# A written order for TensorE and VectorE in the recurrence loop of a hybrid trunk layer

## The chip, the cores and the metric

The kernel runs on one core of a Trainium2 chip. The metric is device time in microseconds (us) for one launch. TensorE is called PE below, VectorE DVE, ScalarE ACT, GpSimd POOL and SyncE SP, as in the profile.

## What is computed

One layer over 256 latent and 256 context tokens, D = 2048, weights in float32. Adaptive modulation from a conditioning vector gives six vectors of 2048 entries; then a bidirectional RWKV-7 time mixing (16 heads of 64) and a convolution branch, merged by two sigmoid gates and projected by `w_o`; then 16 experts that pick 32 tokens each. The recurrence is, per head and direction:

```python
def step(S, inp):
    r_t, k_t, v_t, w_t, kk_t, a_t = inp
    sa = jnp.einsum('bhvk,bhk->bhv', S, kk_t)
    S = (S * w_t[:, :, None, :] - sa[..., None] * (kk_t * a_t)[:, :, None, :]
         + v_t[..., None] * k_t[:, :, None, :])
    y = jnp.einsum('bhvk,bhk->bhv', S, r_t) if emit else None
    return S, y
```

The latent scans start from the context's final states. The merge that the loop's fill work belongs to is

```python
g_r = jax.nn.sigmoid(P[..., OFF_GATE:OFF_GATE + D_MODEL])
g_c = jax.nn.sigmoid(P[..., OFF_GATE + D_MODEL:])
m = (g_r * b_r + g_c * b_c) @ lp['w_o']
```

## The kernel before, in words

The program has four stretches. From 0 to about 548 us come the first modulation vectors and the input projections. From 548 to 1355 us runs the recurrence loop. From 1355 to 1523 us come the output projections. The rest, to 2466 us, is the experts, which stream 2 MB weight tiles.

The loop has 16 units: 8 pairs of heads times 2 directions. `rwkv_dir` (L627) is one unit, a generator cut in five segments by `yield`. All 8 chunks of 64 tokens of a unit are worked on together until the last segment.

- Segment 1 (to L712): loads of keys and the like; two low-rank products (L653, L654); the decays by two scans on DVE (L673, L675, one tile of each is called `Wp`, the other `Wy`), POOL's product `di` of the two (L680), `Wy` from it (L681), and the scaled keys `KB` (L691, DVE) and `VK` (L694, POOL).
- Segment 2 (to L770): score products between keys (L728, masked by DVE into `AT` at L730) and transposes on PE, called flips (L739).
- Segment 3 (to L852): the inverse of 32x32 triangular blocks. DVE first solves two 16x16 blocks by substitution: after gathering into `INP` (L780 to L784) there are 14 steps of two instructions each (L791 or L796 writes `tmp`, L799 subtracts it from `N`), then `OUT` (L801), `TT` (L804) and `T` (L807). The 16x16 blocks are joined by PE products (L812, L819) and one DVE sum (L821, called T2 below) with a transpose (L823), then the 32x32 ones by L832 and L841, and L850 applies scores to values.
- Segment 4 (to L883): L856 applies the inverse to keys and values; products L872 to L876 give the transitions `PT` and `RB` (L880, L882 on DVE).
- Segment 5: seven steps `Z` in a row, in each of which PE multiplies by `PT` (L894) and ACT scales and copies the state back (L895); then the outputs (L899, L903), and, after a second direction, `group_norm` (L929).

Beside the units stand the fills: gate projections, `gate_part` (L553), and modulation parts, `mod_steps` (L258). A fill of the gates splits a weight tile into a high half (ACT, L146, `whi`) and a low half (POOL, L217, `wlo`) and multiplies three times (L221, L222, L223; six matmuls in a fill). A fill of the modulation loads one 1 MB tile `wm` (L263, by SP's queue) and multiplies it in four matmuls (L271). Four such parts make a block; there are eight blocks. There is one `wm` buffer (`MB = 1`). After the fourth part the sum is copied into the same `wm` tile, and `finish` (four matmuls at L288, one DVE sum at L290) reads it from there. It isn't emitted at once but put into the list `later`:

```python
def part(q):
    w = pool.tile([128, n, 512], F32, name="wm", tag="wm", bufs=bufs)
    SP.dma_start(w, w_mod[m, c, :, n * q:n * q + n, :])
```

```python
if pe:
    S["acc"] = w[:, 0]
    (DVE.tensor_copy if MRE else act_copy)(S["acc"], acc)
```

The order before: in each iteration the fills of the unit are emitted by `flush` (L607) with a priority lowered by 1500, and the five segments in the order of the table `ORD` (L45). A scheduler with a simulated timeline then orders every engine's instructions over the whole program; a fill of low priority goes where it expects the engine to be free.

Of the kernel before, what the change touches and what calls it, by code (L numbers as in the profile page):

```python
# [87 lines left out]
for _name, _w in (("ident", 128), ("bones", 128), ("ones", 128), ("mA", 128), ("mM", 128),  # L88
# [40 lines left out]
def kernel(  # L129
# [497 lines left out]
    def rwkv_dir(p, d, bonr, bon, INP):  # L627
# [12 lines left out]
        SP.dma_start(rm, rd[:, p, d])  # L640
        vm = rt("vm", "vm", [512])
        SP.dma_start(vm, vd[:, p, d])
        act_copy(VK[:, 0::3], c8(vm))
        lw = rt("lw", "lw", [2, 128])
# [4 lines left out]
        POOL.tensor_tensor(lwl, lw, lwh, op=OP.subtract)  # L649
        pda = []  # L650
        for r in range(2):
            pda.append(bank("p1"))
            PE.matmul(pda[r], lwh[:, r], zs[d][:, r], start=True, stop=False)  # L653
            PE.matmul(pda[r], lwl[:, r], zs[d][:, r], start=False, stop=True)  # L654
        pd, pa = pda
        w0 = 1 - d
# [9 lines left out]
        ACT.activation(diw, dpw, AF.Exp, scale=-HALF_DECAY, bias=eps[:, 4:5])  # L666
        ACT.activation(dpw, dpw, AF.Exp, scale=HALF_DECAY, bias=eps[:, 3:4])
        Wp = rt("Wp", "a2", [520])
        Wy = rt("Wy", "a2", [520])
# [9 lines left out]
        WC = Wv[:, :, 64 if d == 0 else 0]  # L679
        POOL.tensor_tensor(di, Wp, Wy, op=OP.mult)  # L680
        DVE.scalar_tensor_tensor(Wy, di, 2.0, Wy, op0=OP.subtract, op1=OP.mult)  # L681
        Wi = Wy.rearrange("p (c t) -> p c t", t=65)[:, :, w0:w0 + 64]
        ta = rt("ta", "a2", [512])
        ACT.activation(ta, pa, AF.Tanh, scale=0.5, bias=ha0[:, i16:i16 + 1])
        kp = rt("kp", "a2", [512])
        ACT.activation(kp, ta, AF.Identity, scale=hka[:, i16:i16 + 1], bias=oka[:, i16:i16 + 1])
        ACT.activation(ta, ta, AF.Identity, scale=-0.5, bias=eps[:, 5:6])
        POOL.tensor_tensor(kp, kp, km, op=OP.mult)

        def kbh(o, x):  # L690
            DVE.tensor_tensor(o, cp2(c8(x)), cp2(Wi), op=OP.mult)  # L691

        kbh(KBv[:, :, 0::3], kp)
        POOL.tensor_tensor(VKv[:, :, 1:3], cp2(c8(kn)), cp2(Wq), op=OP.mult)  # L694
        POOL.tensor_tensor(ta, ta, kn, op=OP.mult)
        kbh(KBv[:, :, 1:3], ta)
        POOL.tensor_tensor(VKv[:, 2:4, 4:6], cp2(c8(rm)), cp2(Wt[:, 4:8]), op=OP.mult)
        RB = rt("RB", "RB", [4, 64])
        POOL.tensor_copy(cp2(RB), VKv[:, 2:4, 4:6])
        rk = rt("rk", "rm", [256])  # L700
# [10 lines left out]

        yield  # L712
        vbase = lambda c: 3 * c - c % 2
# [21 lines left out]
        def flip(src, base, dst, g):  # L735
# [4 lines left out]
            act_copy(dst[:, 4 * g:4 * g + 4], pt)  # L740

        scores(4, 128)
        flip(VK, vbase, VU, 0)
        flip(VK, vbase, VU, 1)
        scores(0, 64)
        flip(KB, lambda c: 2 * c, KBt, 0)
        flip(KB, lambda c: 2 * c, KBt, 1)
        VU = VU.rearrange("p c (h t) -> p c h t", h=2)
# [20 lines left out]

        yield  # L770
        quads = [(z, slice(32 * z, 32 * z + 32)) for z in range(4)]
# [13 lines left out]
        Nv = N.rearrange("p x (l y) -> p l x y", l=2)  # L785
        for j in range(1, 15):
            n, m = j, 15 - j
            tmp = rt("tmp", "tmp", [2 * 56])[:, 0:2 * n * m]
            if d == 0:
                tv = tmp.rearrange("p (l r s) -> p l r s", l=2, r=m)  # L790
                DVE.tensor_tensor(tv, Nv[:, :, j:j + 1, 0:j].to_broadcast([128, 2, m, n]),  # L791
                                  Nv[:, :, j + 1:16, j:j + 1].to_broadcast([128, 2, m, n]), op=OP.mult)
                o = Nv[:, :, j + 1:16, 0:j]
            else:
                tv = tmp.rearrange("p (l s r) -> p l s r", l=2, r=m)
                DVE.tensor_tensor(tv, Nv[:, :, 0:j, j:j + 1].to_broadcast([128, 2, n, m]),  # L796
                                  Nv[:, :, j:j + 1, j + 1:16].to_broadcast([128, 2, n, m]), op=OP.mult)
                o = Nv[:, :, 0:j, j + 1:16]
            DVE.tensor_tensor(o, o, tv, op=OP.add)  # L799
# [45 lines left out]
        TT = NT8.rearrange("p (c h) t -> p c h t", h=2)  # L845

        pv = q4bank()
        for cp, h, c, q in each():
            tick(0.07)
            mark["pv"] = PE.matmul(pv[hs(q), cp, h], AT[hs(1 - q), c, h], VU[hs(1 - q), c, h], start=True, stop=True)  # L850
        act_copy(VU[:, 8:12], pv)
        yield  # L852
        ku = [bank().rearrange("p (c h x t) -> p c h x t", c=2, h=2, x=2) for j in range(2)]
# [4 lines left out]
        for j in range(2):  # L858
            act_copy(KN[:, 2 * j:2 * j + 2], ku[j][:, :, :, 0])
            for q in range(2):  # L860
                act_copy(VU[hs(q), 4 * j + 1 - q:4 * j + 4 - q:2], ku[j][hs(q), :, :, 1])
        order = list(range(8)) if d == 0 else [3, 2, 1, 0, 7, 6, 5, 4]
        PP = [c8(bank()) for j in range(2)]
# [15 lines left out]
        for j in range(2):  # L879
            DVE.tensor_tensor(PT[:, 2 - j:8 - j:2], PP[j][:, 2 - 2 * j:8 - 2 * j:2], id3, op=OP.add)  # L880
            o = RB[:, j::2] if d == 0 else RB[:, 3 - j::-2]
            DVE.tensor_tensor(o, o, PP[j][:, 5::2], op=OP.add)  # L882
        yield  # L883
        Z = rt("Z", "c2", [8, 64])
# [5 lines left out]
        for i in range(7):  # L890
            c, cn = order[i], order[i + 1]
            if i > 0:
                for h in range(2):
                    PE.matmul(pz[hs(h), c], PT[hs(h), i], Z[hs(h), c], start=False, stop=True, skip_group_check=True)  # L894
            ACT.activation(Z[:, cn], pz[:, c], AF.Copy, scale=WCk[:, c:c + 1])  # L895
        py = c8(bank(ZB[1]))
        for c in order[4:]:
# [6 lines left out]
        yield py.rearrange("p c t -> p (c t)")[:, 0:256]  # L904

# [23 lines left out]
    def group_norm(p, S):  # L929
# [15 lines left out]
        DVE.scalar_tensor_tensor(ys, ys, vec("lng", p), b0, op0=OP.mult, op1=OP.add)  # L945
        PE.matmul(pm[:, 0:256], S["gw"], sgl, start=True, stop=True)
        DVE.scalar_tensor_tensor(ys, ys, vec("lnb", p), pm[:, 0:256], op0=OP.add, op1=OP.mult)
        if p < PD:
            SP.dma_start(ygd[:, p, :], ys)
        else:  # L950
            act_copy(yh[:, p], ys)
            POOL.tensor_tensor(yl[:, p], ys, yh[:, p], op=OP.subtract)

    pairs = list(pairs)
# [3 lines left out]

    def seg(n, i):
        if i >= len(units):  # L960
            return
        p, d = units[i]
        if n == 1:
            if d == 0:
                S[p] = load_pair(p)
            q = S[p]
            gens[i] = rwkv_dir(p, d, q["bonr"], q["bon"], INP)
        r = next(gens[i])
        if n == 5:
            y = r  # L970
            ys = rt("ys", "ys", [256])
            act_copy(ys, y)
            S[p].setdefault("y", []).append(ys)
            if d == 1:
                group_norm(p, S[p])

    with tc.high_priority(offset=-LOWP):
        for f in early:
            f()
    seg(1, 0)  # L980
    seg(2, 0)
    seg(1, 1)
    seg(3, 0)
    seg(2, 1)
    seg(1, 2)
    for i in range(len(units)):
        flush(len(pend))
        pend.extend(fills[i])
        acc[1] = PT_ / len(pend)
        for n, o in ORD:  # L990
            seg(n, i + o)
        with tc.high_priority(offset=-LOWP):
# [3 lines left out]
    flush(len(pend))  # L996
    with tc.high_priority(offset=-LOWP):
# [379 lines left out]
```

## Time and profile before

| what | us |
|---|---|
| median of three timed runs | 2476.83 |
| the three runs | 2467.78, 2476.83, 2491.22 |
| the profiled execution's own time | 2468.45 |
| its span, first to last instruction | 2466.5 |
| mean granted TensorE clock | 0.89 of full speed |
| PE busy, share of the span | 82% |
| DVE, ACT, POOL busy, shares | 41%, 31%, 27% |

Busy times are of one execution. A busy PE isn't PE at its peak, because matmuls are pipelined and their ends are modelled; a row with "x16" is sixteen instructions in a row, with the time of all of them. The granted clock is the share of full speed at which PE was allowed to run; its two levels are 2.4 and 1.2 GHz.

### The profile page before, as it was taken

The page shows a single profiled execution, that of the slowest core. Times are in us where ns is not written, and L with a number is a line of the kernel's source. Part 1 is how long each engine was busy: PE and PEld are TensorE (multiplying, and loading weights), DVE is VectorE, ACT ScalarE, POOL GpSimd, SP SyncE. Part 2 cuts the span into 40 slices and gives each one's busy share as a digit, 9 for nine tenths or more (in the row PEclk, how much of TensorE's full clock was granted, in tenths as well). Part 3 has the DMA queues.
Part 4 walks back from the last instruction along what each step waited for, and adds up shares of the span by engine and source line. Part 5 has one row for each costly group of instructions (what it writes and reads, how often), then busy time and mean ns, then how long its engine had stood idle before and what let it go on. Part 6 is the DMA issues. An engine that isn't in the chain of part 4 may idle for free.

```text
span 2466.5 us, 45093 instructions
## 1 busy us (share of the span) xinstructions
PE 2018.0 (82%) x18730; PEld 1421.7 (58%) x18730; DVE 1007.2 (41%) x2013; ACT 770.0 (31%) x1524; POOL 654.4 (27%) x690
## 2 busy tenths in 40 slices
PE   7998999996788888788897997877777777777765
PEld 3787788885676766666776995433333333333332
DVE  2347989426756664755611543211111111111112
ACT  3255344543555554455543542000000000000002
POOL 1342334335434254363545732000000000000002
PEclk8999999997779898888998998988898888888887
DMA  9958766674114234243356886999999999999995
GB/s 383 334 184 274 245 200 237 211 236 147 60 54 134 80 131 141 82 148 110 129 193 194 265 295 279 428 428 427 428 426 428 428 428 428 428 427 428 428 417 214
DMA packets 147212, 674.14 MB, mean 273 GB/s; under 512 B 17600, under 2 KB 38208, under 8 KB 109888
## 3 DMA queue, kind: packets, MB, share of 16 engines
q1 hardware_dynamic: 129488, 459.68, 50.8%
q10 hardware_dynamic: 17520, 211.58, 20.4%
q8 instruction: 147, 2.41, 0.4%
q14 instruction: 57, 0.47, 0.1%
HBM read 649.38 MB, written 21.82 MB: 272 GB/s over the span
## 4 chain that ended last, share of the span: by engine, by line
DMA 30%; PE 25%; DVE 7%; ACT 3%; issue 2%; POOL 2%; SPq 0%; ACTq 0%; DVEq 0%; POOLq 0%
DMA wx<-in_w_gu 16%; DMA wx<-in_w_dn 11%; PE rw L1219 2%; PE big L223 2%; DVE N L799 2%; PE big L1256 2%; PE big L221 2%; PE big L222 2%; PE p L1288 2%; PE rw L223 2%; PE rw L221 2%; PE rw L222 1%; PE rw L1248 1%; DMA wraw<-in_w_in 1%; DVE tmp L796 1%
## 5 line engine op out<-in xcount | busy, mean ns | idle before, releaser
L217 POOL TENSOR_TENSOR wlo<-wraw,whi 128x512 fp32r<-128x512 f32 x292 | 398.3, 1369 | 575.9 <-ACT whi L146 452.5
L1256 PE MATMUL big<-wx,xse 128*32 128x512 f32 x2048 | 303.6, 728 | 161.6 <-DMA wx<-in_w_gu 159.7
L146 ACT ACTIVATE whi<-wraw 128x512 fp32r<-128x512 f32 x428 | 263.1, 627 | 402.0 <-DMA wraw<-in_w_in 146.8
L221 PE MATMUL big<-hh,whi 128*128 128x256 f32 x912 | 275.6, 302 | 24.5 <-ACT whi L146 9.4
L223 PE MATMUL big<-hh,wlo 128*128 128x256 f32 x912 | 274.2, 301 | 10.9 <-POOL wlo L217 10.9
L1256 PEld LDWEIGHTS big<-wx,xse 128*32 128x32 f32 x2048 | 63.7, 122 | 362.2 <-DMA wx<-in_w_gu 193.3
L222 PE MATMUL big<-hl,whi 128*128 128x256 f32 x912 | 269.8, 296 | 0.0
L1232 POOL TENSOR_TENSOR r<-r 128x256 f32<-128x256 f32 x11 | 8.2, 746 | 922.1 <-ACT r L1228 921.6
L221 PEld LDWEIGHTS big<-hh,whi 128*128 128x128 f32 x912 | 184.3, 202 | 53.4 <-issue 17.8
L223 PEld LDWEIGHTS big<-hh,wlo 128*128 128x128 f32 x912 | 183.5, 201 | 24.9 <-POOL wlo L217 12.8
L1269 ACT ACTIVATE th<-big 128x256 f32<-128x256 f32 x16 | 6.1, 383 | 588.3 <-PE big L1256 511.9
L222 PEld LDWEIGHTS big<-hl,whi 128*128 128x128 f32 x912 | 184.3, 202 | 6.6 <-issue 4.3
L1270 DVE SCALAR_TENSOR_TENSOR th<-th,big 128x256 f32<-128x256 f32 x16 | 6.7, 421 | 413.8 <-ACT th L1269 413.8
L1223 DVE SCALAR_TENSOR_TENSOR x<-rw,modT,x 128x256 f32<-128x256 f32 x256 | 111.3, 479 | 130.1 <-PE rw L1219 130.0
L217 DVE TENSOR_TENSOR wlo<-wraw,whi 128x512 fp32r<-128x512 f32 x136 | 118.1, 873 | 112.2 <-ACT whi L146 100.3
L1219 PE MATMUL rw<-oT,ye 128*128 128x256 f32 x512 | 134.1, 406 | 30.3 <-ACT ye L146 29.6
L466 DVE SCALAR_TENSOR_TENSOR cv<-up,hcw,cv 128x256 f32<-128x256 f32 x240 | 148.3, 619 | 9.2 <-ACT cv L464 1.0
L221 PE MATMUL rw<-hh,whi 128*128 128x256 f32 x512 | 148.5, 292 | 2.6 <-ACT whi L146 2.6
L223 PE MATMUL rw<-hh,wlo 128*128 128x256 f32 x512 | 147.5, 289 | 3.5 <-POOL wlo L217 3.5
L222 PE MATMUL rw<-hl,whi 128*128 128x256 f32 x512 | 146.9, 288 | 0.0
L1219 PEld LDWEIGHTS rw<-oT,ye 128*128 128x128 f32 x512 | 96.6, 199 | 80.5 <-ACT ye L146 66.7
L1248 PEld LDWEIGHTS rw<-oh,xk 128*128 128x128 f32 x1024 | 123.2, 194 | 32.4 <-issue 29.2
(355 smaller groups left out, 3887.9 us busy)
## 6 DMA issues: line engine op xcount, KB each, us to landing
wx<-in_w_gu ACTq DMA_DIRECT2D x66, 2048.0 KB, 39.1
wx<-in_w_gu SPq DMA_DIRECT2D x61, 2048.0 KB, 39.1
wm<-in_w_mod SPq DMA_DIRECT2D x96, 1024.0 KB, 7.1
wraw<-in_w_in SPq DMA_DIRECT2D x300, 256.0 KB, 4.4
wx<-in_w_dn ACTq DMA_DIRECT2D x32, 2048.0 KB, 38.2
wx<-in_w_dn SPq DMA_DIRECT2D x31, 2048.0 KB, 37.9
wraw<-in_w_o SPq DMA_DIRECT2D x64, 256.0 KB, 6.1
wraw<-in_w_co SPq DMA_DIRECT2D x32, 256.0 KB, 3.0
```

The lines of the kernel that those rows point to most:

```text
L146: return ACT.activation(o, i, AF.Copy, scale=scale)
L217: (POOL if LO[0] < LO[1] else DVE).tensor_tensor(lo, raw, hi, op=OP.subtract)
L221: PE.matmul(o, hi, xh, start=start, stop=False, skip_group_check=True)
L222: PE.matmul(o, hi, xl, start=False, stop=False, skip_group_check=True)
L223: PE.matmul(o, lo, xh, start=False, stop=stop, skip_group_check=True)
L466: DVE.scalar_tensor_tensor(o, up[:, :, j:j + 64], hcw[:, i * KC + j:i * KC + j + 1], o, op0=OP.mult, op1=OP.add)
L799: DVE.tensor_tensor(o, o, tv, op=OP.add)
L1219: PE.matmul(pq[:, 256 * q:256 * q + 256], y[:, 128 * q:128 * q + 128], oT, start=True, stop=True)
L1223: DVE.scalar_tensor_tensor(x, pq[:, 256 * q:256 * q + 256], modT[:, 5, k + q, 0:1], x, op0=OP.mult, op1=OP.add)
L1248: PE.matmul(pxs[:, k], xk[:, s, k], oh[:, s, e], start=(s == 0), stop=(s == 1))
L1256: PE.matmul(pg[32 * j:32 * j + 32, :], xs[:, k, :], w[:, a:a + 512], start=(k == 0), stop=(k == KD - 1))
L1288: PE.matmul(pd[32 * j:32 * j + 32, u], aT[:, 128 * b + 32 * j:128 * b + 32 * j + 32], w[:, 2 * j + b, u], start=(b == 0), stop=(b == 1))
```

## The change

The segments of `rwkv_dir` are cut finer, with named yields, and `PLAN` gives each name a time in us and a unit offset. In iteration i the entries of the plan for units i, i+1, i+2 and i+3 and the unit's about 20 fills, spread evenly over 36 us, are sorted by time and emitted in that order. All of this stands in a manual block for PE and DVE: on these two engines the instructions keep the order in which they are emitted; ACT, POOL and SP are still ordered by the scheduler. The prologue (the first segments of units 0 to 2) stands ahead of the block, and has only the few fills of the list `early`; the remaining fills are emitted inside the block, and no longer at a lowered priority.

Within a unit some work changes place: the two low-rank products are written apart (`lora_mm`), the load of `vm` comes later, the ACT and POOL work on `ta` and `kp` comes ahead of the scans, and the flips of `VK` come ahead of the scores. `group_norm` becomes a part of the same generator. The number of instructions of each kind on each engine stays.

```diff
+PLAN = [(0, 0, "B0"), (4.5, 0, "B1"), (6.5, 0, "Z0"), ..., (18.5, 0, "Z6"),
...
+        (0.1, 1, "A0"), (6.2, 1, "A0b"), (11, 1, "A1"), (19.2, 1, "A2"), (22, 1, "A4"), (25.5, 1, "A5"), (28, 1, "A6"), (29, 1, "A7")]
...
+def MANUAL(nc):
+    return {nc.tensor.engine, nc.vector.engine}
...
         for j in range(1, 15):
+            if j in (5, 10):
+                yield "A0" if j == 5 else "A0b"
...
             ACT.activation(Z[:, cn], pz[:, c], AF.Copy, scale=WCk[:, c:c + 1])
+            yield "Z%d" % i
...
+    run(0, "D6")
+    run(0, "C5")
+    run(1, "D6")
+    run(0, "A7")
+    run(1, "C5")
+    run(2, "D6")
+
+    def fill(f):
+        while later and f in modf:
+            later.pop(0)()
+        f()
+
+    with tc.manual_schedule(engines=MANUAL(nc)):
+        for i in range(len(units)):
+            n = len(fills[i])
+            todo = [(t, run, (i + o, s)) for t, o, s in PLAN] + [(F0 + F1 * (j + 0.5) / n, fill, (f,)) for j, f in enumerate(fills[i])]
+            for t, f, a in sorted(todo, key=lambda x: x[0]):
+                f(*a)
```

In the plan the letter D is segment 1, C segment 2, A segment 3, B and Z segments 4 and 5, G the group norm. A name's rows end at its yield: "A1" ends with `T` (L807), "A2" holds L812, "A4" holds L819 and T2. Line numbers of the changed kernel differ: the gates' L221 to L223 are L231 to L233 there, L271 is L281, L288 is L298, L728 is L747, L739 is L758, L894 is L926, L673 is L694, L681 is L702, L691 is L706, L799 is L825, L801, L804 and L807 are L827, L830 and L833, L821 is L849.

PE before, around the finish of one block (`p_8001<-C,wm`, L288); `hh_92` and `hl_93` are the two halves of the tokens, so those rows are gate fills:

```order
L850 MATMUL rw<-VU,AT 64x64 x16
L856 MATMUL rw<-VU,NT_7682 64x128 x16
L288 MATMUL p_8001<-C,wm 128x1 x4
L221 MATMUL big<-hh_92,whi 128x256
L222 MATMUL big<-hl_93,whi 128x256
L223 MATMUL big<-hh_92,wlo 128x256
L221 MATMUL big<-hh_92,whi 128x256
L889 MATMUL gn<-VU,KM 64x64 x14
L653 MATMUL p_8458<-zs_1397,lwh 128x512
```

The next part (L271) follows thirty-three rows after this finish. PE now, at the start of a block: the finish of the block before (L298) and the first part of the next (L281) stand next to each other.

```order
L747 MATMUL rw<-VK,KB 128x128 x8
L926 MATMUL gn<-Z,PT 64x64 x2
L298 MATMUL p_8950<-C,wm 128x1 x4
L281 MATMUL big<-wm,slp 32x512 x4
L661 MATMUL p_8963<-zs_1398,lwh 128x512
L662 MATMUL p_8963<-zs_1398,lwl 128x512
L231 MATMUL big<-hh_92,whi 128x256
L232 MATMUL big<-hl_93,whi 128x256
L233 MATMUL big<-hh_92,wlo 128x256
```

Some rows later in the same block, on PE now, between its second part and its third:

```order
L281 MATMUL big<-wm,slp 32x512 x4
L926 MATMUL gn<-Z,PT 64x64 x2
L758 MATMUL rw<-C,KB 128x128 x4
L231 MATMUL big<-hh_92,whi 128x256
L232 MATMUL big<-hl_93,whi 128x256
L233 MATMUL big<-hh_92,wlo 128x256
L231 MATMUL big<-hh_92,whi 128x256
L232 MATMUL big<-hl_93,whi 128x256
L233 MATMUL big<-hh_92,wlo 128x256
L926 MATMUL gn<-Z,PT 64x64 x2
L281 MATMUL big<-wm,slp 32x512 x4
```

The parts of a block are a few PE rows apart now, always the same.

DVE before, after one unit's substitution:

```order
L801 STREAM_TRANSPOSE OUT<-N 128x512
L804 TENSOR_TENSOR TT<-OUT,C 128x256
L807 STREAM_TRANSPOSE T<-TT 128x256
L880 TENSOR_TENSOR PT<-rw,con_idb 128x3x64
L882 TENSOR_TENSOR RB<-RB,rw 128x2x64
L880 TENSOR_TENSOR PT<-rw,con_idb 128x3x64
L882 TENSOR_TENSOR RB<-RB,rw 128x2x64
L290 TENSOR_TENSOR modT<-p_9192,V 128x4
L821 TENSOR_TENSOR T_10073<-T,sb 128x256
L823 STREAM_TRANSPOSE TT<-T_10073 128x256
L673 SCALAR_TENSOR_TENSOR Wp<-dp,C 128x520
L673 SCALAR_TENSOR_TENSOR Wy<-di,C 128x520
```

DVE now, at the same place of a unit:

```order
L827 STREAM_TRANSPOSE OUT<-N 128x512
L830 TENSOR_TENSOR TT<-OUT,C 128x256
L833 STREAM_TRANSPOSE T<-TT 128x256
L749 TENSOR_TENSOR AT<-rw,C 128x4x64 x2
L694 SCALAR_TENSOR_TENSOR Wp<-dp,C 128x520
L694 SCALAR_TENSOR_TENSOR Wy<-di,C 128x520
L702 SCALAR_TENSOR_TENSOR Wy<-di,Wy 128x520
L706 TENSOR_TENSOR KB<-kp,Wy 128x4x2x64
L706 TENSOR_TENSOR KB<-ta,Wy 128x4x128
L849 TENSOR_TENSOR T_10389<-T,sb 128x256
L851 STREAM_TRANSPOSE TT<-T_10389 128x256
```

The scans, `Wy` and both `KB` of a later unit stand ahead of T2 now, where T2 stood ahead of them.

## Rows read from the trace of the kernel before

**Rows 1.** Busy times by stretch; columns are named in the first line.
```profile
core 0: us, PE busy (x) PEld busy (x) DVE busy (x) ACT busy (x) POOL busy (x), PEclk, DMA share, GB/s
548.00:650.00 102.00, 71.99 (x789) 58.18 (x791) 63.71 (x111) 43.95 (x84) 52.94 (x56) 0.77 0.41 132
650.00:1250.00 600.00, 496.36 (x7436) 406.70 (x7427) 362.86 (x776) 315.16 (x676) 264.00 (x274) 0.86 0.35 111
1250.00:1355.00 105.00, 88.02 (x773) 76.38 (x772) 10.70 (x17) 43.15 (x87) 53.53 (x44) 0.90 0.62 193
1355.00:1523.00 168.00, 149.05 (x1229) 142.89 (x1227) 82.13 (x132) 78.61 (x151) 91.76 (x84) 0.95 0.80 281
```

**Rows 2.** PE's longest waits from 548 to 1355: total us, times, longest.
```profile
PE sb L812 <- DVE T L807: 33.7, 6, 6.9
PE gn L894 <- DVE PT L880: 23.3, 3, 8.8
PE rw L728 <- DVE KB L691: 16.3, 6, 7.0
PE big L223 <- POOL wlo L217: 11.1, 9, 3.8
...
PE big L271 <- DMA wm<-in_w_mod: 6.9, 5, 2.5
```

**Rows 3.** Single lines of PE: ns min/median/max, first to last start in us.
```profile
L856 PE MATMUL rw<-VU,NT x512: 268/269/473, 628.0 to 1260.3; 64*64 64x128 f32 x171
L653 PE MATMUL p<-zs,lwh x32: 390/502/797, 551.1 to 1185.0; 128*128 128x512 f32 x32
```

**Rows 4.** Timeline around one load of `wm`: start, us, engine, line.
```profile
1155.19 0.33 SPq L263 DMA_DIRECT2D wm<-in_w_mod  x1
...
1160.79 1.08 PE L271 MATMUL big<-wm,slp 128*32 128x512 f32 x4
```

**Rows 5.** The loads of `wm` from 548 to 1355, issue to landing.
```profile
DMA to landing us min/median/max: 4.8/5.1/7.8
```

**Rows 6.** Timeline of PE, single rows; the last two at half clock.
```profile
1018.94 0.28 PE L221 MATMUL big<-hh,whi 128*128 128x256 f32 x1
1019.06 0.28 PE L222 MATMUL big<-hl,whi 128*128 128x256 f32 x1
...
1019.30 0.60 PE L739 MATMUL rw<-C,VK 128*128 128x128 f32 x4
...
1024.11 0.75 PE L819 MATMUL sb<-Q,TT 32*32 32x32 f32 x64
...
1034.21 0.68 PE L903 MATMUL gn<-RB,Z 64*64 64x64 f32 x16
...
1051.87 0.41 PE L222 MATMUL big<-hl,whi 128*128 128x256 f32 x1
1052.08 0.41 PE L223 MATMUL big<-hh,wlo 128*128 128x256 f32 x1
...
1156.05 0.33 PE L894 MATMUL gn<-Z,PT 64*64 64x64 f32 x4
```

**Rows 7.** A PE row of the scores.
```profile
576.78 1.11 PE L728 MATMUL rw<-VK,KB 64*128 64x64 f32 x16
```

**Rows 8.** POOL's groups, 650 to 1250: busy us, mean ns, idle before, releasers.
```profile
L217 POOL TENSOR_TENSOR wlo<-wraw,whi 128x512 fp32r<-128x512 f32 x99 | 130.3, 1321 | 180.0 <-ACT whi L146 137.5 <-PE big L223 30.2 <-PE p L653 4.3
L694 POOL TENSOR_TENSOR VK<-kn,Wp 128x512 f32<-128x512 f32 x13 | 23.1, 1776 | 32.1 <-DVE Wp L675 24.3 <-PE rw L728 6.5 <-DVE Wp L673 1.4
```

**Rows 9.** DVE's substitution, 650 to 1250: one group of it.
```profile
L799 DVE TENSOR_TENSOR N<-N,tmp 128x28 f32<-128x28 f32 (+6 forms) x196 | 75.7, 386 | 6.0
```

**Rows 10.** DVE and POOL side by side in the substitution, timeline.
```profile
1038.09 0.28 DVE L799 TENSOR_TENSOR N<-N,tmp 128x112 f32<-128x112 f32 x1
...
1038.71 1.31 DVE L799 TENSOR_TENSOR N<-N,tmp 128x112 f32<-128x112 f32 x1
```
**Rows 11.** POOL at the same time.
```profile
1038.63 1.26 POOL L217 TENSOR_TENSOR wlo<-wraw,whi 128x512 fp32r<-128x512 f32 x1 [3.27 <-ACT whi L146]
```

**Rows 12.** Two more stretches of 20 us, columns as in rows 1.
```profile
588.00:608.00 20.00, 7.91 (x50) 7.13 (x51) 18.86 (x30) 2.88 (x5) 13.38 (x15) 0.64 0.33 99
...
968.00:988.00 20.00, 16.68 (x157) 12.03 (x154) 8.50 (x12) 7.17 (x17) 14.04 (x15) 0.91 0.72 241
```

More of the change, by code (lines that the diff above doesn't have):

```diff
@@ L73 @@
 LOWP = 1500
+F0, F1 = 0.5, 36.0
+PLAN = [(0, 0, "B0"), (4.5, 0, "B1"), (6.5, 0, "Z0"), (8.5, 0, "Z1"), (10.5, 0, "Z2"), (12.5, 0, "Z3"), (14.5, 0, "Z4"), (16.5, 0, "Z5"), (18.5, 0, "Z6"),
[4 rows of a table added]
 MODS = [8]
@@ L640, in rwkv_dir @@
         SP.dma_start(rm, rd[:, p, d])
-        vm = rt("vm", "vm", [512])
-        SP.dma_start(vm, vd[:, p, d])
-        act_copy(VK[:, 0::3], c8(vm))
         lw = rt("lw", "lw", [2, 128])
@@ L649, in rwkv_dir, with lora_mm @@
         POOL.tensor_tensor(lwl, lw, lwh, op=OP.subtract)
[L650 to L655, printed above, removed]
+        yield "D0"
+        def lora_mm(r):
+            o = bank("p1")
+            PE.matmul(o, lwh[:, r], zs[d][:, r], start=True, stop=False)
+            PE.matmul(o, lwl[:, r], zs[d][:, r], start=False, stop=True)
+            return o
+        pd = lora_mm(0)
         w0 = 1 - d
@@ L667, in rwkv_dir @@
         ACT.activation(dpw, dpw, AF.Exp, scale=HALF_DECAY, bias=eps[:, 3:4])
+        yield "D1"
+        pa = lora_mm(1)
+        ta = rt("ta", "a2", [512])
+        ACT.activation(ta, pa, AF.Tanh, scale=0.5, bias=ha0[:, i16:i16 + 1])
+        kp = rt("kp", "a2", [512])
+        ACT.activation(kp, ta, AF.Identity, scale=hka[:, i16:i16 + 1], bias=oka[:, i16:i16 + 1])
+        ACT.activation(ta, ta, AF.Identity, scale=-0.5, bias=eps[:, 5:6])
+        POOL.tensor_tensor(kp, kp, km, op=OP.mult)
+        yield "D2"
         Wp = rt("Wp", "a2", [520])
@@ L680, in rwkv_dir @@
         POOL.tensor_tensor(di, Wp, Wy, op=OP.mult)
+        POOL.tensor_tensor(ta, ta, kn, op=OP.mult)
+        yield "D3"
         DVE.scalar_tensor_tensor(Wy, di, 2.0, Wy, op0=OP.subtract, op1=OP.mult)
         Wi = Wy.rearrange("p (c t) -> p c t", t=65)[:, :, w0:w0 + 64]
[L683 to L688, printed above, removed]
         def kbh(o, x):
             DVE.tensor_tensor(o, cp2(c8(x)), cp2(Wi), op=OP.mult)
+        yield "D4"
+        vm = rt("vm", "vm", [512])
+        SP.dma_start(vm, vd[:, p, d])
+        act_copy(VK[:, 0::3], c8(vm))
         kbh(KBv[:, :, 0::3], kp)
+        kbh(KBv[:, :, 1:3], ta)
         POOL.tensor_tensor(VKv[:, :, 1:3], cp2(c8(kn)), cp2(Wq), op=OP.mult)
-        POOL.tensor_tensor(ta, ta, kn, op=OP.mult)
-        kbh(KBv[:, :, 1:3], ta)
         POOL.tensor_tensor(VKv[:, 2:4, 4:6], cp2(c8(rm)), cp2(Wt[:, 4:8]), op=OP.mult)
@@ L701, in rwkv_dir @@
         POOL.tensor_tensor(rk, rm, kp[:, 256:512], op=OP.mult)
+        yield "D5"
         pb = bank("p1")
@@ L710, in rwkv_dir @@
         POOL.tensor_copy(WCk, WC)
-        yield
+        yield "D6"
         vbase = lambda c: 3 * c - c % 2
@@ L740, in flip @@
             act_copy(dst[:, 4 * g:4 * g + 4], pt)
+        flip(VK, vbase, VU, 0)
+        yield "C0"
+        flip(VK, vbase, VU, 1)
+        yield "C1"
         scores(4, 128)
-        flip(VK, vbase, VU, 0)
-        flip(VK, vbase, VU, 1)
+        yield "C2"
         scores(0, 64)
+        yield "C3"
         flip(KB, lambda c: 2 * c, KBt, 0)
+        yield "C4"
         flip(KB, lambda c: 2 * c, KBt, 1)
@@ L768, in mm_all @@
                 PE.matmul(o[hs(q), cp, h], l[hs(q), cp, h], r[hs(q), cp, h], start=True, stop=True)
-        yield
+        yield "C5"
         quads = [(z, slice(32 * z, 32 * z + 32)) for z in range(4)]
@@ L807, in rwkv_dir @@
         DVE.transpose(T, TT)
+        yield "A1"
         pq = c8(bank("sb"))
@@ L814, in rwkv_dir @@
         act_copy(Q, pq[:, :, 0:32])
+        yield "A2"
         pq = c8(bank("sb"))
@@ L826, in rwkv_dir @@
             act_copy(NT8[:, :, 32 * l:32 * l + 32], TT, mh[:, l:l + 1])
+        yield "A4"
         e, o = (0, 32) if d == 0 else (32, 0)
@@ L836, in rwkv_dir @@
             act_copy(Q[b:b + 32], pq[b:b + 32, :, 0:32])
+        yield "A5"
         pq = c8(bank("sb"))
@@ L845, in rwkv_dir @@
         TT = NT8.rearrange("p (c h) t -> p c h t", h=2)
+        yield "A6"
         pv = q4bank()
@@ L851, in rwkv_dir @@
         act_copy(VU[:, 8:12], pv)
-        yield
+        yield "A7"
         ku = [bank().rearrange("p (c h x t) -> p c h x t", c=2, h=2, x=2) for j in range(2)]
@@ L861, in rwkv_dir @@
                 act_copy(VU[hs(q), 4 * j + 1 - q:4 * j + 4 - q:2], ku[j][hs(q), :, :, 1])
+        yield "B0"
         order = list(range(8)) if d == 0 else [3, 2, 1, 0, 7, 6, 5, 4]
@@ L882, in rwkv_dir @@
             DVE.tensor_tensor(o, o, PP[j][:, 5::2], op=OP.add)
-        yield
+        yield "B1"
         Z = rt("Z", "c2", [8, 64])
@@ L903, in rwkv_dir @@
                 PE.matmul(py[hs(h), c - 4], Z[hs(h), c], RB[hs(h), c - 4], start=False, stop=True, skip_group_check=True)
-        yield py.rearrange("p c t -> p (c t)")[:, 0:256]
+        ys = rt("ys", "ys", [256])
+        act_copy(ys, py.rearrange("p c t -> p (c t)")[:, 0:256])
+        S[p].setdefault("y", []).append(ys)
+        yield "B2"
+        if d == 1:
+            yield from group_norm(p, S[p])
     mark = {}
@@ L936, in group_norm @@
         pm = bank(GNB)
+        yield "G0"
         PE.matmul(pm[:, 0:256], bones, ys, start=True, stop=True)
@@ L940, in group_norm @@
         ACT.activation(sq, ys, AF.Square)
+        yield "G1"
         PE.matmul(pm[:, 256:512], bones, sq, start=True, stop=True)
@@ L945, in group_norm @@
         DVE.scalar_tensor_tensor(ys, ys, vec("lng", p), b0, op0=OP.mult, op1=OP.add)
+        yield "G2"
         PE.matmul(pm[:, 0:256], S["gw"], sgl, start=True, stop=True)
@@ L952, in group_norm @@
             POOL.tensor_tensor(yl[:, p], ys, yh[:, p], op=OP.subtract)
+        yield "G3"
     pairs = list(pairs)
@@ L957, with run @@
     gens = {}
-    def seg(n, i):
+    def run(i, last):
         if i >= len(units):
@@ L962, in seg @@
         p, d = units[i]
-        if n == 1:
+        if i not in gens:
             if d == 0:
                 S[p] = load_pair(p)
[L966 to L975, printed above, removed]
+            gens[i] = rwkv_dir(p, d, S[p]["bonr"], S[p]["bon"], INP)
+        if last[0] == "G" and d == 0:
+            return
+        while next(gens[i]) != last:
+            pass
     with tc.high_priority(offset=-LOWP):
@@ L979 @@
             f()
[L980 to L992, printed above, removed]
+    run(0, "D6")
[14 more added lines that the diff above has]
+                f(*a)
             if i >= 16 - len(REL):
@@ L995 @@
                     reload_y(slice(a, a + 2))
-    flush(len(pend))
     with tc.high_priority(offset=-LOWP):
```

3 rows, old and new, of the table PLAN are left out of this document.

## The prediction

> **What bounds the kernel now.** I began with the busy times by stretch [rows 1]. The recurrence loop runs from 548 to 1355, 807 us. PE is busy 72.0 + 496.4 + 88.0 = 656.4 us of it and idle 150.6; DVE, ACT and POOL are all far below that, so PE is nearest to being the bound, with waits in between. Weighted by length the granted clock there is (102 x 0.77 + 600 x 0.86 + 105 x 0.90) / 807 = 0.854. Next the rows of one line in every unit: L856 starts first at 628.0 and last at 1260.3 [rows 3], fifteen units later, so a unit takes 42.1 us. Then PE's waits [rows 2]: the long ones are for DVE, 33.7 us for the result `T` of the substitution, 23.3 for `PT`, 16.3 for `KB`, in a few places of up to 8.8 us each, while most units have none of them. The wait for `wm` is only 6.9 us. The stretch after the loop has PE busy 149 of 168 us [rows 1] and needs the loop's whole result, so I pass a gain or loss of the loop on to the end in full.
>
> PE's work scales with its clock: two neighbouring gate matmuls start 0.12 us apart at full clock (1018.94 and 1019.06) and 0.21 us apart at the half level (1051.87 and 1052.08) [rows 6].
>
> **The change part by part.** Nothing is removed or added on any engine; only places change. So the sum is new idle time of PE against the old 150.6, and the clock.
>
> *The load of `wm`.* The finish of a block now stands directly ahead of the first part of the next on PE, and there is one buffer that the finish reads. The next load can be issued only after the finish, and PE's next row needs it. In the trace, issue to first matmul is 1160.79 - 1155.19 = 5.6 us [rows 4], of which landing takes 5.1 in the median [rows 5]. Before, some thirty PE rows, mostly gate fills, covered that. Now PE waits 5.6 us there, with everything queued behind it: the low-rank products, gates, scores and the `Z` steps. Between the parts of a block stands some work too. Priced at full clock: a gate fill is six matmuls of 0.12, 0.7 us; a `Z` product 0.33, a flip 0.60, sixty-four small joining products 0.75, sixteen output products 0.68 [rows 6]; sixteen score products 1.11 [rows 7]; a low-rank pair about 2 x 0.5 = 1.0 [rows 3]. Between parts 1 and 2 stand a pair, two gate fills, two `Z`, half a set of scores and a flip, 4.7 us; between 2 and 3 two `Z`, a flip, a gate fill, 2.0; between 3 and 4 about a `Z`, the joining products, a gate fill and both output products, 3.1. The waits left are 0.9, 3.6 and 2.5, so 12.6 us a block with the first. Eight blocks, the first without its finish: 7 x 12.6 + 7.0 = 95 us. Bounds: if PE is late for other reasons, only the first wait of a block stays, 7 x 5.6 = 39; if every load took the longest landing of 7.8 instead of 5.1, 95 + 31 x 2.7 = 179. I take 95, the row nearest to it being the median.
>
> *Units without a block.* The other eight units, and what is not covered in the rest, depend on DVE and POOL. DVE is busy 362.9 us in 600, which at 42.1 a unit is 25.5 us a unit [rows 1]. In the written order the scans, `Wy` and both `KB` of a later unit stand ahead of T2, and the plan puts T2's segment at 22 us. Some 2 us of the 25.5 stand behind T2 (group norm, gates), so T2 comes 1 to 2 us late. POOL's order isn't written, but it is in order: `VK` waited 24.3 us in 13 instances for a DVE scan, 1.9 each, and any `wlo` (1.3 us each) queued behind it is late for a gate fill of PE [rows 8], which now can't be passed. I take 1.5 + 1.9 + 1.3, about 5 us, for each of eight units: 40. Bounds: 0 (the plan leaves room, as many units before had no such wait) and 16 x 6.9 = 110, every unit with the longest wait for `T` [rows 2].
>
> For DVE a substitution step of 112 columns takes 0.28 us alone, and 1.31 while a POOL split of 1.26 runs beside it [rows 10, 11]; the mean is 386 ns [rows 9], so the sum above has the collisions in it. The Trainium skill, *Perfetto Trace Analysis*, section *Optimizing Scalar/DVE Operations*, says that GpSimd and DVE share an SBUF read port, which a two-port DVE instruction locks for itself; the pair of rows agrees that one holds up the other. By that rule no written order of DVE alone can keep its slots, since POOL's rows fall where they like; three more collisions in a unit's 22 us would be 3 us more, 24 over the eight units, where the mean of the rows gives nothing more.
>
> *Start and end.* In the prologue the gate and modulation fills are gone apart from the early ones. From the first low-rank product at 551.1 to the first L856 at 628.0 are 77 us [rows 3]; without fills between I estimate 62, since POOL's and ACT's splits no longer stand in that chain; PE has some 20 us of its own work there, so 42 us idle, against 102 - 72 = 30 for 548 to 650 before [rows 1]. At the end, before, left-over fills keep PE busy 88 of 105 us, 17 idle; I take 15 now. Bounds for both together: 30 and 75.
>
> *The clock.* The stretches show 0.77 with 29% idle, 0.86 with 17%, 0.90 with 16%, 0.95 with 11% [rows 1]. Within the loop, 20 us with PE idle 12.1 have 0.64 and 20 us with 3.3 idle have 0.91 [rows 12]. The new order has more idle time, which speaks for a lower clock, but in pieces of 5.6 us at most instead of 7 to 9, and fills spread through every unit, which speaks for a higher one. I take 0.90, that of the stretch in which fills stood evenly: 656.4 x 0.854 / 0.90 = 622.9, a gain of 33.5. Bounds: 0.77 costs 656.4 x 0.854 / 0.77 - 656.4 = 72, 0.95 gains 66.
>
> *The sum.* Idle 95 + 40 + 42 + 15 = 192, which is 41 more than 150.6; the clock takes back 33.5. So 8 us more, 2468.45 + 8 = 2476 against the profiled execution. The median of the runs is 8 above that execution, at 2476.83, which would give 2485. I put 2480. About 1% is what a measurement of this kernel can tell from no change; its three runs alone spread over 23 us. So the forecast is no measurable change, by two terms that cancel.
>
> **The rivals.**
>
> *PE follows the plan (faster).* The waits for `wm` fall on places where PE would wait for DVE anyway, or at the half clock, where the 4.7 us of work between parts 1 and 2 take 8. Then the new waits cost the lower part: 55 for `wm`, 30 for the other units, 40 and 15 at the ends, 140 idle in all, 10 less than before; at a clock of 0.91 PE's work is 616, 40 less. That is 50 less: 2420. For it: before, the 73 us of waits for DVE are caused by an order in which DVE's rows of several units lie in an unlucky succession, and the plan spreads them. Against it: the finish directly ahead of the next part is a wait that no plan time removes. Chance 0.33.
>
> *Waits in a fixed order add up (slower).* The mechanism is a T2 that stands behind another unit's scans. If POOL's `di` and `kp`, which DVE waits for ahead of `Wy` and `KB`, are late because splits for the gates stand before them on POOL, T2 is late in every unit and PE, whose rows can't be passed, waits there, in units with a block as in those without. At 5 us in sixteen units instead of eight that is 80, idle 95 + 80 + 57 = 232, 81 more; then the clock hardly rises, 0.88, worth 19. So 62 more: 2531. It decides once T2 starts later than about 25 us after its unit's `INP`, which is where the wait at L841's counterpart begins. For it: POOL is busy 264 of 600 us and waits on ACT for its splits. Against it: at 42 us a unit DVE has 16 us to spare. Chance 0.31.
>
> *The order written is not much other than the scheduler's.* The rows of PE and DVE differ at the places shown, so this I leave within the forecast.
>
> **How the numbers follow.** Forecast, no change within 1%, 0.36: 2480, its own range 2450 to 2510. Faster by over 1% 0.33, slower by over 1% 0.31. The range reaches down to 2415, just past the faster case, and up to 2545, just past the slower one; below it lies the case in which the clock goes to 0.95 and the waits to their lower bounds, above it the one with long landings or a clock under 0.85, about one in ten each.
>
> **What would show it.** In the changed kernel's waits of PE, L281 for `wm` should be the largest, 70 to 110 us, in some 24 to 31 places, with a load issued just after an L298. The wait of L231 to L233 for `wlo` should rise above its 11 us. The long waits for `T`, `PT` and `KB` should fall from 73 us to below 40. The distance of L856 between units should alternate, longer in those with a block. The granted clock from 650 to 1250 should be about 0.90. I am wrong if `wm` costs under 40 us, if T2 waits in every unit, or if the clock in the loop falls to 0.8 or lower.

## The result and the profile after

The changed kernel took 2495.25 us in the median of 18 runs (2482.17 to 2503.12), the kernel before 2475.18 (18 runs, 2461.83 to 2491.22). The ratio is 1.0075, 95% interval 1.0054 to 1.0096: 20 us more, three quarters of a per cent. The profiled execution took 2497.85 us with a span of 2496.1, 29.6 more than before's 2466.5. One execution of ten of a kernel below (low-priority fills) took 4559.67 us and is left out of its ratio.

The stretches, with the columns of [rows 1]; the second view has the whole loop, which ends where the first row of L1098 (L1057 before) begins, at 1390 instead of 1357:

```profile
548.00:650.00 102.00, 65.56 (x822) 49.92 (x824) 62.05 (x119) 46.83 (x92) 49.20 (x57) 0.68 0.34 109
650.00:1250.00 600.00, 479.25 (x6636) 385.70 (x6629) 337.28 (x677) 291.81 (x614) 267.47 (x268) 0.84 0.37 117
1250.00:1390.00 140.00, 114.85 (x1550) 98.54 (x1549) 48.28 (x110) 67.22 (x143) 59.50 (x50) 0.93 0.45 141
1390.00:1555.00 165.00, 146.59 (x1224) 140.22 (x1223) 81.12 (x132) 77.97 (x149) 90.20 (x83) 0.95 0.80 283
```

```profile
548.00:1390.00 842.00, 659.66 (x8994) 534.16 (x8995) 447.61 (x905) 405.85 (x847) 376.16 (x374) 0.83 0.38 120
```

Of the kernel before, the same view to 1357:

```profile
548.00:1357.00 809.00, 658.36 (x8992) 543.09 (x8991) 437.35 (x905) 403.10 (x847) 371.76 (x374) 0.86 0.39 125
```

PE is busy as long as before (659.7 against 658.4). The loop is 33 us longer, and PE's idle time in it 842.0 - 659.7 = 182.3 instead of 150.6, so 32 more: the difference is idle time of PE in the loop. What comes after the loop is 3 us shorter (1106.1 against 1109.5). The loop's granted clock is 0.83 instead of 0.86.

PE's waits from 540 to 1400, the same view as [rows 2]:

```profile
PE big L281 <- DMA wm<-in_w_mod: 90.7, 28, 7.3
PE gn L976 <- DVE ys L969: 25.1, 6, 5.1
PE sb L839 <- DVE T L833: 16.3, 6, 4.0
PE rw L758 <- POOL VK L714: 10.8, 2, 5.8
PE rw L747 <- DVE tmp L817: 7.7, 1, 7.7
...
PE rw L747 <- DVE KB L706: 4.1, 1, 4.1
PE big L233 <- POOL wlo L227: 3.6, 4, 1.8
...
PE gn L926 <- DVE PT L912: 1.7, 1, 1.7
```

The wait for `wm` went from 6.9 us to 90.7 and is the largest by far. The three waits for DVE that led before (`T` 33.7, `PT` 23.3, `KB` 16.3) are 16.3, 1.7 and 4.1. The wait for the group norm's sum `ys` rose from 10.1 us to 25.1; before it was

```profile
PE gn L937 <- DVE ys L931: 10.1, 3, 5.8
```

One block of the modulation in the timeline of PE; in brackets the idle time ahead and what ended it:

```profile
1113.32 1.05 PE L298 MATMUL p<-C,wm 128*128 128x1 f32 x8 [0.86 <-ACT ta L681]
1119.36 1.93 PE L281 MATMUL big<-wm,slp 128*32 128x512 f32 x8 [4.98 <-DMA wm<-in_w_mod]
1126.34 1.94 PE L281 MATMUL big<-wm,slp 128*32 128x512 f32 x8 [0.75 <-DMA wm<-in_w_mod]
1134.55 1.06 PE L281 MATMUL big<-wm,slp 128*32 128x512 f32 x8 [2.17 <-DMA wm<-in_w_mod]
1142.49 1.47 PE L281 MATMUL big<-wm,slp 128*32 128x512 f32 x8 [4.06 <-DMA wm<-in_w_mod]
```

The finish, then nothing at all until the load lands, then the first part; and shorter waits at the other three. 12.0 us in this block. (The timeline counts an L281 twice, so "x8" are the four matmuls of a part.) The first part after the wait ran at the half level, a granted clock of 0.50:

```profile
1119.40:1121.20 1.80, 1.80 (x8) 0.16 (x8) 1.68 (x3) 0.00 (x0) 0.00 (x0) 0.50 0.01 2
```

What the half clock does to the row after such a wait is seen in the matmuls of `wm` themselves, loop only (ns min/median/max), before and after:

```profile
L271 PE MATMUL big<-wm,slp x256: 592/617/1061, 557.7 to 1317.4; 128*32 128x512 f32 x128
```

```profile
L281 PE MATMUL big<-wm,slp x256: 592/1057/1063, 622.2 to 1326.2; 128*32 128x512 f32 x128
```

The median went from 617 ns, near the full level, to 1057, the half one.

### The profile page after: what moved, and what is told of

Same layout as the page of the kernel before. It is cut to its first block, busy times and chain, and to the rows that moved or that the text cites. A ratio compares the mean times of both kernels' runs of the same rounds, so it can differ in the third digit from the quotient of the medians.

```text
span 2496.1 us, 45084 instructions
## 1 busy us (share of the span) xinstructions
PE 2010.4 (81%) x18730; PEld 1407.3 (56%) x18730; DVE 1016.5 (41%) x2013; ACT 773.4 (31%) x1524; POOL 657.3 (26%) x690
## 4 chain that ended last, share of the span: by engine, by line
DMA 33%; PE 13%; POOL 2%; ACT 2%; issue 1%; DVE 1%; SPq 0%; ACTq 0%; DVEq 0%; POOLq 0%
DMA wx<-in_w_gu 15%; DMA wx<-in_w_dn 14%; PE rw L1260 2%; DMA wm<-in_w_mod 1%; PE p L1329 1%; DMA wraw<-in_w_o 1%; PE big L1297 1%; PE rw L1289 1%; PE gn L1329 1%; PE big L231 1%; POOL wlo L227 1%; PE rw L231 1%; PE rw L233 1%; PE rw L232 1%; DMA wraw<-in_w_ro 1%
## 5 line engine op out<-in xcount | busy, mean ns | idle before, releaser
L231 PE MATMUL big<-hh,whi 128*128 128x256 f32 x912 | 285.5, 313 | 3.4 <-ACT whi L156 3.4
L233 PE MATMUL big<-hh,wlo 128*128 128x256 f32 x912 | 263.7, 289 | 2.6 <-POOL wlo L227 1.8
L232 PE MATMUL big<-hl,whi 128*128 128x256 f32 x912 | 263.0, 288 | 0.0
L231 PEld LDWEIGHTS big<-hh,whi 128*128 128x128 f32 x912 | 179.4, 197 | 31.1 <-issue 17.7
L233 PEld LDWEIGHTS big<-hh,wlo 128*128 128x128 f32 x912 | 179.5, 197 | 6.0 <-POOL wlo L227 3.4
L233 PE MATMUL rw<-hh,wlo 128*128 128x256 f32 x512 | 147.5, 289 | 3.8 <-POOL wlo L227 3.8
L231 PE MATMUL rw<-hh,whi 128*128 128x256 f32 x512 | 148.4, 292 | 2.7 <-ACT whi L156 2.7
```

The lines of the kernel that those rows point to most:

```text
L231: PE.matmul(o, hi, xh, start=start, stop=False, skip_group_check=True)
L232: PE.matmul(o, hi, xl, start=False, stop=False, skip_group_check=True)
L233: PE.matmul(o, lo, xh, start=False, stop=stop, skip_group_check=True)
```

## The experiments

Theory A: the new waits for the one `wm` buffer stand on PE's path and are paid in full. Rival B: PE would be late there anyway, for DVE and POOL, and other waits take their place. Times below are medians; the kernel before had 2470 to 2473 in these comparisons, and ratios are to it.

**The finish earlier, then the parts spread.** The first run moves the finish; the second also sets the spacing of a block's parts from 0.15 to 0.9 of two units.

```diff
     def fill(f):
-        while later and f in modf:
+        if later and f not in modf:
+            wait_f[0] += 1
+        if later and (wait_f[0] >= 2 or f in modf):
             later.pop(0)()
+            wait_f[0] = 0
         f()
...
+    wait_f = [0]
```

```diff
-MSP = 0.15
+MSP = 0.9
```

> The changed kernel with the finish of a modulation block emitted two fills after the block's last part, instead of directly ahead of the next block's first part; nothing else differs. Theory A (the waits for the one load buffer stand on PE's path and are paid in full): the first wait of a block, 5.6 us, goes in seven blocks, 39 us, so about 2456 against 2495 for the changed kernel, and PE's wait for wm falls from 90.7 to about 50. Rival B (PE would be late there anyway, for DVE and POOL): the wait for wm falls as much, but the time stays within 12 us of 2495, and the waits for T, VK or the group norm's ys rise instead.

> As the run before, and the four parts of a block are spread over two units, one after about ten fills, instead of all within the first third of one unit. Theory A: no part waits any more, the 90.7 us of PE's wait for wm fall below 10, and the time to about 2410, faster than the kernel before. Rival B: wm's wait goes, and other waits take at least half of it, so 2440 or more. Rival C (the clock): idle time falls as in A, but the clock of the loop stays at 0.83, so that PE's busy time is as before and the time ends near 2430.

Measured: 2459.65 us (ratio 0.9939, 0.9914 to 0.9964) and 2408.17 (0.9739, 0.9719 to 0.9759). Theory A had said 2456 and 2410. In the first, PE's wait for `wm`:

```profile
PE big L281 <- DMA wm<-in_w_mod: 66.3, 23, 6.3
```

It fell by only 24 us, not 39: the first wait is gone, but PE comes to the other three parts sooner and waits there 66.3 us instead of 52.6 (up to 6.3 each). The time fell by 36. In the profiled executions the loop is 43 us shorter, by 26 of PE's idle time and by 17 of its busy time (659.7 to 642.7). In the second run PE has no wait for `wm` at all. The loops of the two, with the columns of [rows 1]:

```profile
548.00:1347.00 799.00, 642.72 (x8998) 524.54 (x8997) 462.36 (x905) 404.31 (x848) 376.27 (x374) 0.85 0.39 127
```

```profile
548.00:1305.00 757.00, 636.66 (x9000) 524.28 (x9000) 464.51 (x905) 403.86 (x848) 379.06 (x375) 0.87 0.41 134
```

Rival B and rival C (no gain by the clock) both fail. But that 87 us came back for 90.7 of waits is in part luck: PE's idle time fell by 62 only (182.3 to 120.3), as other waits took some 29 us, above all `AT` and `gtt` (20.4 and 13.1), and its busy time fell by 23. So theory A holds for the time, and in this run about two thirds of the waits came back as idle time.

**Loads taken away, order kept.** The change is in `part`, for the loop's blocks alone.

```diff
-            w = pool.tile([128, n, 512], F32, name="wm", tag="wm", bufs=bufs)
-            SP.dma_start(w, w_mod[m, c, :, n * q:n * q + n, :])
+            if q == 0 or later is None:
+                S["w"] = pool.tile([128, n, 512], F32, name="wm", tag="wm", bufs=bufs)
+                SP.dma_start(S["w"], w_mod[m, c, :, n * q:n * q + n, :])
+            w = S["w"]
...
```

> The changed kernel with its order untouched, but only the first part of a loop's modulation block is loaded; the other three multiply the same tile, so the last four modulation vectors come from wrong weights. Theory A: PE's waits at parts 2 to 4 go, about 65 of the 90.7 us, and the time falls by at least as much, to 2415 to 2435; what falls beyond the waits is the clock's. Rival B (other waits come in their place): 2460 or more, with the waits for T, ys and VK up by 30 us or more. 24 MB fewer of DMA are no part of either, since the DMA engines are busy less than 0.4 of the loop.

Measured: 2437.94 (0.9853, 0.982 to 0.9887), 57 us less than the changed kernel, a few us short of theory A's interval. Its waits:

```profile
PE big L283 <- DMA wm<-in_w_mod: 38.0, 7, 7.1
PE gn L978 <- DVE ys L971: 24.5, 6, 5.1
PE sb L841 <- DVE T L835: 16.2, 6, 4.0
```

What is left is the first wait of seven blocks, 38.0 / 7 = 5.4 us each, close to the price read from one load (5.6) [rows 4]. The wait fell by 52.7 and the time by 57; the waits for `ys` and `T` did not move. The loop:

```profile
548.00:1335.00 787.00, 649.17 (x9006) 529.48 (x9005) 449.86 (x905) 405.66 (x848) 382.15 (x380) 0.84 0.31 98
```

PE's idle time is 137.8 of it, 44.5 less, and its busy time 10.5 less. That PE's written order turned hidden loads into waits is shown twice, by moving the loads and by taking them away.

**Which engine's order.** The list of engines in `MANUAL`, or the block itself:

```diff
-    return {nc.tensor.engine, nc.vector.engine}
+    return {nc.tensor.engine}
...
-    return {nc.tensor.engine, nc.vector.engine}
+    return {nc.vector.engine}
...
-    with tc.manual_schedule(engines=MANUAL(nc)):
+    with ExitStack():
```

> The changed kernel with only PE in the written order; DVE is left to the scheduler. Theory A: PE's order holds the waits for wm, so they stay at 80 to 100 us and the time stays within 15 us of 2495; the wait for the group norm's ys (25 us) may shrink. Rival (DVE's written order causes the loss): the time returns to about 2475 or below.

> The changed kernel with only DVE in the written order; PE is left to the scheduler. Theory A: the finish and the next part come apart again on PE, wm's wait falls to under 30 us, and the time is at or below the kernel before, 2450 to 2480. Rival (DVE's written order causes the loss): 2490 or more, with PE waiting for T, PT and ys.

> The changed kernel without the manual block: the plan's cut and order of emission and the fills at normal priority, but PE and DVE both ordered by the scheduler. Theory D (DVE's written order is what gains): the gain of the vector-only run, 2407, is lost, so 2450 to 2480. Rival E (the finer plan and the fills' priority gain, the written order of DVE nothing): within 15 us of 2407.

Measured: PE's order alone 2493.32 (1.009, 1.0073 to 1.0107), DVE's alone 2407.03 (0.9736, 0.9703 to 0.9768), none 2407.00 (0.9731, 0.9698 to 0.9764). In the run with PE's alone, `wm` holds 84.7 us again:

```profile
PE big L281 <- DMA wm<-in_w_mod: 84.7, 28, 9.6
PE rw L747 <- DVE RB L914: 31.6, 10, 5.0
```

and with DVE's alone 9.3:

```profile
PE big L281 <- DMA wm<-in_w_mod: 9.3, 9, 2.3
```

So with the parts close together PE's written order costs 86 to 88 us whether DVE's is written or not, DVE's costs and gains nothing, theory D falls and rival E holds. For DVE's order alone theory A had the wait right (under 30) and the time wrong, 2450 to 2480: it held nothing for the rest of the change. That rest, the plan's cut and order of emission with fills at normal priority, gains about 65 us by itself: PE's idle time in the loop is 740.0 - 670.8 = 69 us there, against 150.6 before. The small result of the whole change is a gain of 65 and a loss of 88.

**What the 65 us are.** Without written order, the fills go back to lowered priority:

```diff
     def fill(f):
-        while later and f in modf:
-            later.pop(0)()
-        f()
+        with tc.high_priority(offset=-LOWP):
+            while later and f in modf:
+                later.pop(0)()
+            f()
...
```

> As the run without written order (2407), but the fills keep the priority lowered by 1500 that they have in the kernel before. Theory P (the fills' normal priority at their planned place gains): the gain goes, 2460 to 2480. Rival Q (the finer cut of the units and its order gain): stays at 2407, within 12 us.

Measured: 2463.43 (0.9946, 0.9913 to 0.9978). Of the 65 us, about 56 belong to the fills' priority at their planned place and some 8 to the finer cut and its order (5 to 21 by the interval). Theory P holds. In the profiled executions the loop is 68 us longer than without the lowered priority (808 against 740), half of it idle time of PE (103 against 69) and half busy time (705 against 671, at a clock of 0.84 against 0.88). By what steps the lowered priority does this wasn't followed.

**Spread parts with fewer written orders.** The same two edits as in the second run, with DVE's order alone, none, and PE's alone; and the spacing alone in the kernel before.

> DVE alone in the written order, with the finish two fills after the last part and the four parts spread over two units. Theory A: there PE waited only 9.3 us for wm, so it gains at most 10 us more than the vector-only run: 2395 to 2410. Rival (the scheduler had put the loads well, and spread parts come late or use PE at worse places): 2415 or more.

> No written order at all, finish early and parts spread. If DVE's written order does nothing, this equals the run with it, 2378, within 10 us. Rival (it helps once the loads are out of the way): 2390 or more.

> PE alone in the written order, DVE left to the scheduler, finish early and parts spread. With both orders this was 2408, with DVE's alone 2378, with none 2374. Theory F (a fixed order of PE costs by itself, since no row can pass one that waits for DVE, ACT or POOL): 2400 to 2415, as with both. Rival G (the two fixed orders hold each other up): 2390 or less.

> The kernel before with only the spread of a block's parts over two units. Before, PE waited 6.9 us for wm in the loop, so by theory A at most that is gained: 2462 to 2475. Rival (the four parts close together cost more than their waits, in priority or in clock): 2450 or less.

Measured: DVE alone 2377.61 (0.9622, 0.9586 to 0.9657); none 2373.62 (0.9619, 0.9586 to 0.9652); PE alone 2370.47 (0.9586, 0.9536 to 0.9636); the kernel before with spread parts 2433.22 (0.985, 0.9816 to 0.9884).

That none equals DVE alone within 10 us came as said. Two theories failed. First, spreading (without written order for PE together with the early finish) gains 29 to 39 us even where PE waited only 7 to 11 us for `wm`: theory A's bound was too tight, twice, and the rival that close parts cost more than their waits holds. In the kernel before, PE's idle time fell from 150.6 to 123.7 and its longest waits with it:

```profile
PE sb L812 <- DVE T L807: 26.0, 6, 9.6
PE big L221 <- DVE gtt L572: 16.6, 4, 7.3
PE gn L894 <- DVE PT L880: 10.1, 2, 5.6
PE big L271 <- DMA wm<-in_w_mod: 9.5, 4, 3.2
PE rw L728 <- DVE KB L691: 8.4, 3, 4.8
```

The wait for `wm` is no smaller; `T`, `PT` and `KB` are (33.7, 23.3 and 16.3 before), while the gates' `gtt` rose from 7.9. What the close parts did to those was not tried. Second, theory F fails: PE's written order costs nothing by itself once the loads are spread, and neither does DVE's; both together cost 2408.17 - 2370.47 = 38 us. So the price belongs to the two orders together, as rival G said. In the profiled executions the loop with PE's order alone is 43 us shorter than with both, 33 of them idle time of PE (120.3 against 87.4):

```profile
548.00:1262.00 714.00, 626.56 (x8995) 518.12 (x8996) 454.21 (x905) 404.80 (x847) 384.53 (x374) 0.89 0.44 141
```

PE's waits from 650 to 1250, both orders:

```profile
PE rw L758 <- DVE AT L749: 20.4, 5, 4.3
PE gn L976 <- DVE ys L969: 14.6, 4, 3.9
PE sb L839 <- DVE T L833: 13.3, 7, 3.0
```

and PE's alone:

```profile
PE rw L747 <- DVE tmp L822: 9.4, 3, 3.4
PE rw L747 <- DVE RB L914: 6.3, 6, 2.5
```

DVE's own waits in that stretch with both orders:

```profile
DVE PT L912 <- PE rw L906: 38.8, 8, 8.7
DVE Wy L702 <- POOL di L699: 35.5, 12, 3.1
```

and with DVE's order alone:

```profile
DVE PT L912 <- PE rw L906: 48.8, 8, 14.5
DVE Wy L702 <- POOL di L699: 40.3, 12, 4.2
```

With both written, DVE stands 74 us ahead of `PT` and `Wy`, one of them for PE, and PE 48 us for `AT`, `ys` and `T`; with DVE free, these three waits are no longer among PE's larger ones. DVE's waits by themselves are no price: with its order alone written they are longer, 89 us, and the time is 2377.61, since there PE's waits for the three are 7.7 us. A reading that fits is that a DVE held at `PT` or `Wy` leaves rows that PE needs standing behind, and that a PE in fixed order has nothing else to do meanwhile. That those rows were ready in each case wasn't followed one by one, so this step is argued and not shown.

**More fills in the prologue.** In the version with both orders and spread parts, 24 early parts instead of 12:

```diff
-EARLY = 1
+EARLY = 2
```

> PE and DVE in the written order, finish early and parts spread as in that run (2408), and twice as many gate fills in the prologue, where PE sat idle 36 of 102 us. Theory: the 12 fills more are 72 matmuls, 9 to 15 us of work taken out of the loop and hidden there, so 2393 to 2400. Rival: they delay the prologue's own chain by their splits on ACT and POOL, and the time stays within 5 us of 2408 or goes above.

Measured: 2417.76 (0.9774, 0.974 to 0.9807), 10 us more. A miss: the fills moved to the prologue did not pay. They hardly touched its idle time: from 548 to 650 PE is busy 67.9 us at a clock of 0.77, where without them it was 66.2 at 0.65. The waits for the gates' `gtt` and for T2, 13.1 and 3.1 us without the change, rose:

```profile
PE big L231 <- DVE gtt L582: 31.7, 10, 7.5
PE sb L861 <- DVE T L849: 25.7, 7, 5.4
```

All gates come earlier in the written order and so meet DVE at other places; that this causes the waits wasn't tried.

The fastest versions, 2370 to 2378, beat the kernel before by about 4%; between the three the intervals don't decide.

## Why the prediction was right or wrong

The forecast was no change within 1%, 2480 us with a range to 2545; measured 2495, inside its own range of 2450 to 2510. Against the profiled execution it said 8 us more, and 29.4 were measured. The idle time was right in its largest term, and one of the two terms that were to cancel did not come, so that the forecast held is in part luck: by its idle time alone, without the gain by the clock, it would have forecast 41 us more, over 1%. And the 0.75% measured stand clear of no change (interval 0.54 to 0.96%).

- *The load of `wm`*: 95 us, measured 90.7 in 28 waits. The first wait was put at 5.6 and is 5.4 in seven blocks; in the block shown the four are 4.98, 0.75, 2.17, 4.06 where 5.6, 0.9, 3.6, 2.5 were worked out. The sum is right, the third and fourth wait are off in opposite directions. The experiments show that it costs about its size in time.
- *Units without a block, start and end*: 40 + 42 + 15 = 97, measured 182.3 - 90.7 = 92. The start, 548 to 650, is idle 102 - 65.6 = 36.4. But inside the 40 the cause was another, so that this term came out by luck. It was to be T2 and `wlo`; the wait for `wlo` fell from 11.1 to 3.6 us instead of rising, and PE has no wait for T2. What stands there, in six of the eight units without a block, is `ys` (25.1), which I didn't name, and a smaller `T` (16.3), together 41.4. The distance between units alternates as said: from the third L887 (L856 before) at 700 us to the fourteenth at 1256, 49 to 56 us with a block and 46 to 47 without.
- *Idle in all*: 192 forecast, 182 measured.
- *The clock* is the step that failed, in sign: 0.90 and 33.5 us back were forecast; it is 0.83 (0.84 from 650 to 1250), and PE's busy time didn't fall (659.7 against 658.4). I weighed shorter pieces of idle time against more of it, and chose the shorter pieces; in all seven blocks that begin with a wait of about 5 us, the part behind it ran at the half level. (In [rows 6] the rows at half clock are the two at 1051.87 and 1052.08; the last row ran at full clock.) Scaling all busy time with the mean clock failed as well: over all these runs, the loop's busy time lies between 627 and 671 us at clocks from 0.83 to 0.93, in no order with the clock (the run with low-priority fills, 705 at 0.84, stands apart, and why stays open).
- *The faster rival* was right that `T`, `PT` and `KB` would shrink (73 to 22 us) and wrong that the new waits would fall on old ones. *The slower rival*'s T2 in every unit didn't come. In *The rivals* I took the plan and the written order for one thing; the runs show a gain of 65 us in the one and a loss of 88 in the other, and I foresaw neither as such. The loss is the term for `wm`; the gain stands in the working only as less idle time outside the waits for `wm`, 97 us instead of 150.6 - 6.9 = 143.7, and what brings it, the fills' priority, isn't named.

On the rule of the Trainium skill's *Perfetto Trace Analysis*, section *Optimizing Scalar/DVE Operations*, no run here separates the shared port from the rest, since each keeps POOL's and DVE's rows. DVE's written order alone cost nothing (2407.03 against 2407.00) and didn't stretch DVE's work: it is busy 448.3 us in the loop with its order written and 449.1 without. With both orders it is 447.6 against 437.4 in the kernel before, 10 us more where the working had 24 by that rule.

## What to carry to other kernels

Where an engine's order is written by hand, look for each load into a single buffer at where the row that frees it stands against the row that needs the next load: the work between the two must be longer than the load takes, and the trace of the kernel before gives both. Test a plan of emission apart from the fixing of orders, and the orders one engine at a time: here the plan gained 65 us, one order next to nothing either way with the loads spread, and two orders together cost 38. With the loads close together PE's order cost 86 to 88. A second `wm` buffer (`MB = 2`), the other way to hide these loads, was not tried.

## What wasn't expected of the hardware

The clock. The same `wm` matmuls ran at 617 ns in the median before and 1057 behind the new waits, and the granted clock of the loop fell with 32 us more idle time from 0.86 to 0.83. With the loads spread and no written order it was 0.92, and the loop 713 us long, with 713.0 - 653.3 = 59.8 idle; its row, columns of [rows 1]:

```profile
548.00:1261.00 713.00, 653.25 (x9040) 542.02 (x9039) 439.07 (x904) 404.79 (x847) 385.44 (x380) 0.92 0.44 141
```

Yet PE's busy time was nearly the same in both, 659.7 and 653.3. The mean granted clock of the loop did not tell here how long the work takes, though single rows did take longer at the half level; what made up for them in the sum wasn't followed.
